# Delta rule: 16-row diagonal blocks inverted together on VectorE, doubling from 16 rows; convolution taps on VectorE alone

## The chip, the cores and the metric

The kernel runs on one core of one Trainium2 chip. The metric is the device time of one execution in microseconds; three executions of the kernel before gave 2950.22, 2953.05 and 2955.62 us, median 2953.05 us. Profiles are of one execution. The engines go by the profile's names: PE is TensorE's matmul, PEld its weight load, DVE is VectorE, ACT ScalarE, POOL GpSimd, SP SyncE (here: the queue that issues nearly all DMAs).

## What is computed

Two layers of a diffusion block (512 latent and 256 context tokens of width 1024: latent attention, a conformer branch with a 31-tap depthwise convolution, a short convolution, an MLP of width 4096), then two layers of a hybrid block on 512 tokens: gated delta rule, pooling and sparse attention, three branches with gates. All in float32. The change is in the first block's convolutions and in the delta rule:

```python
lmat = where(strict, einsum('nbhid,nbhjd->nbhij', k_beta, kc) * decay, 0)
tmat = triangular_solve(eye + lmat, eye, lower=True, unit_diagonal=True)
u = einsum('nbhij,nbhjd->nbhid', tmat, v_beta)
w = einsum('nbhij,nbhjd->nbhid', tmat, k_beta * exp(gc)[..., None])
```

and, of the conformer branch, `u = a * sigmoid(g)`, then a depthwise convolution with 31 taps plus a bias, a layer norm and a SiLU. The reference takes chunks of 64 rows; the kernel takes 4 chunks of 128 rows for each of 4 heads.

## The kernel before, in words

Matmuls of the projections run as three products of float32r parts: every weight tile is loaded by SP into a raw buffer, ACT casts it to the high part (`split`, L335) and DVE, or POOL where `pool=True`, subtracts to get the low part (L336). `fm` (L371) multiplies one 128-column weight tile with all tokens in 8 steps of three products (L382); `mm3` (L365) does the same for other products (L367 to L369). Matmuls on plain float32 data show as two records each.

The order of the work is made in three stages. Generators yield their own cost, and `Weave` (L211) runs whichever has the smallest clock, each at a rate of its own. A rehearsal of the whole program gives buffers their places. Then the framework's scheduler sets the order within each engine's queue; each engine and SP take their queue in that order, and semaphores carry the waits between them.

**First block.** For each layer `conv_proj` (L739) makes ten products, two times two for the gated input of the 31-tap convolution (`u`, L760) and two times three for the short convolution (L784 to L793). Each product loads and splits its own weight tile just before its matmuls; in the three-part loop the subtract is on POOL. `conv_taps` (L800) does the taps of two groups of 128 channels, 798 columns wide in layer 0 and 512 in layer 1: 24 of 30 taps as one multiply-add on DVE (L822); every fifth goes as a scaled copy on ACT (L815), which POOL adds up (L819), and one add on DVE (L824) joins them. Taps, projection and attention are woven at L1309, the taps at rate 1.1.

**Second block.** In each layer `second_layer` (L1967) weaves a chain, delta rule and then sparse attention at rate 1.25, with the choice of keys (`select_keys`, a long row of DVE instructions) and with `fill`: delta inputs, pooling, `sparse_proj` 0, `gated` of branch 1, `sparse_proj` 1, `gated` 0, `gated` 2. `delta` (L1555) takes the four chunks in turn. `head(n)` (L1569) transposes k and q, makes decay factors (L1585 to L1590) and the strictly lower matrix `Lw` (L1602), for four heads side by side as [128, 4, 128]. POOL then multiplies `Lw` with seven masks (L1609), one for each doubling level of block size 1, 2, 4 to 64. The inverse starts as identity minus level 0 on DVE (L1706). Each of six further levels does, for four heads, X minus Y times (Lm times X): four matmuls (L1719), a copy on ACT (L1720), four matmuls (L1725), a subtract on DVE (L1726), and, but for the last, a transpose of X into Y, four transposes (L1711) and a copy (L1712). While chunk n doubles, the head of chunk n+1 and the step of chunk n-1 (`step`, which uses the inverse and carries the state) are run between its pieces (`aside`). What each piece takes on the chain's clock stands in `STEPS` (L1553).

## Time and profile before

| | |
|---|---|
| median of three executions | 2953.05 us (2950.22 to 2955.62) |
| profiled execution | 2958.29 us, span of its instructions 2956.2 us |
| PE busy | 2824.0 us, 96% of the span |
| DVE busy | 1657.3 us, 56% |
| ACT busy | 1164.2 us, 39% |
| POOL busy | 576.7 us, 20% |
| granted PE clock, mean | 0.981 |

A row of instructions names line, engine, operation, output and inputs, shape and count, then busy time, mean duration and the engine's idle time ahead of them with what ended it. Durations of matmuls overlap, since they are pipelined: the cost of one is read from the distance between starts. A line number is that of the kernel before unless said otherwise; the changed kernel's lines stand one to some hundred further down.

### The profile page before, as it was taken

The page shows a single profiled execution, that of the slowest core. Times are in us where ns is not written, and L with a number is a line of the kernel's source. Part 1 is how long each engine was busy: PE and PEld are TensorE (multiplying, and loading weights), DVE is VectorE, ACT ScalarE, POOL GpSimd, SP SyncE. Part 2 cuts the span into 40 slices and gives each one's busy share as a digit, 9 for nine tenths or more (in the row PEclk, how much of TensorE's full clock was granted, in tenths as well). Part 3 has the DMA queues.
Part 4 walks back from the last instruction along what each step waited for, and adds up shares of the span by engine and source line. Part 5 has one row for each costly group of instructions (what it writes and reads, how often), then busy time and mean ns, then how long its engine had stood idle before and what let it go on. Part 6 is the DMA issues. An engine that isn't in the chain of part 4 may idle for free. (4 is left out here: it accounts for less than half of the span.)

```text
span 2956.2 us, 39081 instructions
## 1 busy us (share of the span) xinstructions
PE 2824.0 (96%) x15247; PEld 2341.5 (79%) x15247; DVE 1657.3 (56%) x2705; ACT 1164.2 (39%) x2260; POOL 576.7 (20%) x726
## 2 busy tenths in 40 slices
PE   6989999999999889999999999899999999999999
PEld 4867777888888767778888777798888878888887
DVE  4785652333334696554444787574543786675542
ACT  5337643222222527643233544343332543343431
POOL 2434220000000243210000124420311033412211
PEclk9989999999999889999999999999999999999999
DMA  6233344322121423542322511233233410232332
GB/s 218 56 96 121 119 162 132 93 59 77 58 62 58 131 76 108 185 139 83 96 86 92 155 44 30 61 83 90 72 105 99 136 34 24 65 95 72 87 107 79
DMA packets 319329, 276.62 MB, mean 94 GB/s; under 512 B 16868, under 2 KB 260776, under 8 KB 319144
## 3 DMA queue, kind: packets, MB, share of 16 engines
q1 hardware_dynamic: 318170, 271.90, 30.6%
q8 instruction: 120, 1.97, 0.3%
q0 software_dynamic: 704, 2.13, 0.2%
q14 instruction: 65, 0.53, 0.1%
q10 hardware_dynamic: 270, 0.09, 0.0%
HBM read 258.06 MB, written 13.66 MB: 92 GB/s over the span
## 5 line engine op out<-in xcount | busy, mean ns | idle before, releaser
L382 PE MATMUL bank<-at_r,at_r 128*128 128x512 f32 (+1 forms) x5568 | 1233.4, 376 | 18.6 <-POOL at_r L336 7.0
L382 PEld LDWEIGHTS bank<-at_r,at_r 128*128 128x128 f32 x5568 | 966.3, 191 | 201.0 <-issue 8.3
L336 DVE TENSOR_TENSOR at_r<-at_f,at_r 128x1024 fp32r<-128x1024 f32 (+5 forms) x436 | 476.0, 1098 | 467.1 <-ACT at_r L335 346.7
L367 PE MATMUL bank<-at_r,at_r 128*128 128x512 f32 (+5 forms) x1832 | 669.3, 366 | 17.8 <-DVE at_r L495 12.3
L335 ACT CAST at_r<-at_f 128x1024 fp32r<-128x1024 f32 (+6 forms) x450 | 414.2, 929 | 677.3 <-PE bank L369 176.1
L368 PE MATMUL bank<-at_r,at_r 128*128 128x512 f32 (+5 forms) x1832 | 658.9, 360 | 0.1
L369 PE MATMUL bank<-at_r,at_r 128*128 128x512 f32 (+5 forms) x1832 | 657.3, 359 | 0.0
L367 PEld LDWEIGHTS bank<-at_r,at_r 128*128 128x128 f32 x1832 | 349.4, 191 | 91.4 <-issue 15.1
L368 PEld LDWEIGHTS bank<-at_r,at_r 128*128 128x128 f32 x1832 | 350.4, 191 | 47.2 <-DVE at_r L336 1.4
L369 PEld LDWEIGHTS bank<-at_r,at_r 128*128 128x128 f32 x1832 | 349.4, 191 | 47.9 <-issue 1.0
L448 POOL MEMSET at_f<- 128x1 f32 x34 | 3.0, 98 | 873.7 <-PE bank L382 840.1
L515 POOL TENSOR_SCALAR at_f<-at_f,mx 128x768 f32<-128x768 f32 (+3 forms) x112 | 88.5, 791 | 364.6 <-DVE mx L514 335.7
L1217 DVE TENSOR_TENSOR at_f<-at_f,bank 128x512 f32<-128x512 f32 x120 | 81.7, 687 | 108.2 <-PE bank L369 108.2
L1172 ACT ACTIVATE at_f<-bank 128x768 f32<-128x768 f32 (+1 forms) x64 | 45.1, 704 | 202.5 <-PE bank L382 202.5
L1176 DVE TENSOR_TENSOR at_f<-at_f 128x768 f32<-128x768 f32 (+1 forms) x64 | 52.6, 822 | 89.8 <-ACT at_r L1175 89.8
L1609 POOL TENSOR_TENSOR at_f<-at_f,at_f 128x512 f32<-128x512 f32 x56 | 85.2, 1556 | 35.0 <-DVE at_f L1602 35.0
L512 DVE TENSOR_REDUCE mx<-bank 128x1 f32<-128x768 f32 (+1 forms) x80 | 67.4, 847 | 28.9 <-PE bank L369 28.7
L1952 POOL TENSOR_TENSOR at_f<-at_f 128x512 f32<-128x512 f32 x32 | 47.0, 1468 | 184.3 <-DVE at_f L1951 165.9
L336 DVE TENSOR_TENSOR at_r<-bank,at_r 128x256 fp32r<-128x256 f32 (+3 forms) x124 | 59.2, 483 | 35.5 <-ACT at_r L335 34.9
L822 DVE SCALAR_TENSOR_TENSOR at_f<-at_f,at_f 128x798 f32<-128x798 f32 x48 | 73.7, 1553 | 0.9
L513 ACT ACTIVATE at_f<-bank,mx 128x768 f32<-128x768 f32 (+1 forms) x80 | 65.6, 821 | 13.7 <-DVE mx L512 13.1
L335 ACT CAST at_r<-bank 128x256 fp32r<-128x256 f32 (+3 forms) x124 | 51.7, 424 | 46.5 <-PE bank L369 12.8
(292 smaller groups left out, 3233.9 us busy)
## 6 DMA issues: line engine op xcount, KB each, us to landing
at_f<-in_w_in_dram SPq DMA_DIRECT2D x148, 512.0 KB
at_f<-in_w_mod_dram SPq DMA_DIRECT2D x96, 512.0 KB
at_f<-in_w_mlp_in_dram SPq DMA_DIRECT2D x64, 512.0 KB
at_f<-in_w_mlp_out_dram SPq DMA_DIRECT2D x64, 512.0 KB
at_f<-d SPq DMA_DIRECT2D x28, 512.0 KB
at_f<-in_w_branch_dram SPq DMA_DIRECT2D x48, 256.0 KB
d<-at_f SPq DMA_DIRECT2D x22, 512.0 KB
at_f<-in_w_o_dram SPq DMA_DIRECT2D x16, 512.0 KB
```

What stands on the lines that cost most here:

```text
L335: self.nc.scalar.copy(hi, src)
L336: (self.nc.gpsimd if pool else self.nc.vector).tensor_tensor(lo, src, hi.bitcast(F32), op=OP.subtract)
L367: mm(ps, L[1], R[0], start=start, stop=False)
L368: mm(ps, L[0], R[1], start=False, stop=False)
L369: mm(ps, L[0], R[0], start=False, stop=stop)
L382: mm(ps[:, o:o + b - a], w[x][:, k], hl[y][:, k, a:b], start=k == 0 and j == 0, stop=k == nk - 1 and j == 2)
L512: nc.vector.tensor_reduce(mx[:, 0:1], ps, axis=AX, op=OP.max, negate=True)
L513: nc.scalar.activation(P, ps, AF.Exp, bias=mx[:, 0:1], accum_out=mx[:, 1:2])
L515: nc.gpsimd.tensor_scalar(P, P, mx[:, 2:3], 1.0, op0=OP.mult, op1=OP.mult)
L822: nc.vector.scalar_tensor_tensor(a, x, w, a, op0=OP.mult, op1=OP.add)
L1217: nc.vector.tensor_tensor(y, y, ps[t], op=OP.add)
L1609: nc.gpsimd.tensor_tensor(h["Lm"][lv], Lw, B2(self.mk[:, 4 + lv]), op=OP.mult)
```

## The change

Three things change.

The delta rule: the heads of all four chunks run first. Each writes, in 8 DMAs, its sixteen-row diagonal blocks to DRAM (512 runs of 64 bytes a head). One DMA brings the 128 blocks of 16 by 16 back, one block on each partition. Fifteen pairs of DVE instructions invert all of them at once, a copy transposes the result, two DMAs write result and transpose to DRAM, two read them back as [128, 16, 16] (2048 runs of 64 bytes each). `spread` puts them on the diagonal with a mask on POOL, as X and Y of each chunk, and makes the three level masks of block size 16, 32 and 64. The doubling has three levels instead of six after level 0. The clocks of the pieces (`STEPS`, `MOVE`) are larger. The mask table shrinks from 11 to 8.

The convolutions: all 30 taps on DVE at rate 1.6, no ACT copies and no POOL adds. `conv_proj` loads the weight of the next product ahead of the matmuls of this one and splits it after four of its eight steps, always with the subtract on DVE.

The fill: `gated` of branch 1 moves ahead of `sparse_proj` 0.

```diff
     def conv_proj(self, L):
...
+        def fetch():
+            raw, x = self.raw(8, 128), next(units)
+            nc.sync.dma_start(raw, x)
+            return raw
+        ready = [self.parts(fetch())]
+
+        def product():
+            w, ps = ready.pop(), self.P(T)
+            raw = fetch() if len(cols) > 1 else None
+            cols.pop()
+            for n, x in enumerate(self.fm(ps, w, src)):
+                if n == self.SPLIT and raw is not None:
+                    ready.append(self.parts(raw))
+                yield x
+            self.F(w)
+            return ps
...
-                w = self.w_fm(W, 0, 8, col + b * 128, pool=True)
-                ps = self.P(T)
-                yield from self.fm(ps, w, src)
-                self.F(w)
+            for part in range(3):
+                ps = yield from product()
...
             for s in range(1, 31):
-                x, w = u[:, s:s + n], c["cw"][:, s, b:b + 1]
-                if s % self.SIDE == 1 and s < 30:
...
-                nc.vector.scalar_tensor_tensor(a, x, w, a, op0=OP.mult, op1=OP.add)
+                nc.vector.scalar_tensor_tensor(a, u[:, s:s + n], c["cw"][:, s, b:b + 1], a, op0=OP.mult, op1=OP.add)
                 yield n / 960.0
-            nc.vector.tensor_tensor(a, a, side, op=OP.add)
...
-            W = Weave().add(self.conv_taps(L), 1.1).add(proj).add(self.attention(L))
+            W = Weave().add(self.conv_taps(L), 1.6).add(proj).add(self.attention(L))
...
-    STEPS = (0.62, 0.52, 1.35, 0.31)
+    STEPS, MOVE = (1.1, 1.4, 0.9), 4.0
...
-            h["Lm"] = [A() for _ in range(7)]
-            for lv in range(7):
-                nc.gpsimd.tensor_tensor(h["Lm"][lv], Lw, B2(self.mk[:, 4 + lv]), op=OP.mult)
-            F(Lw)
...
+            for b in range(8):
+                q = slice(16 * b, 16 * b + 16)
+                nc.sync.dma_start(rows[0].rearrange("(g b i) j -> b i g j", b=8, i=16)[b][:, 4 * n:4 * n + 4], Lw[q, :, q])
...
+        def blocks():
+
+            Lc, Z, tmp = (self.A(16, 16) for _ in range(3))
+            nc.sync.dma_start(Lc, rows[0].rearrange("(m i) j -> m i j", i=16))
+            nc.gpsimd.memset(Z, 0.0)
+            nc.gpsimd.memset(Z.rearrange("p c i -> p (c i)")[:, 0:256:17], 1.0)
+            yield self.MOVE
+            for i in range(1, 16):
+                nc.vector.tensor_tensor(tmp[:, :i, :i], Z[:, :i, :i], Lc[:, i:i + 1, :i].to_broadcast([128, i, i]),
+                                        op=OP.mult)
+                nc.vector.tensor_reduce(Z[:, :i, i], tmp[:, :i, :i], axis=AX, op=OP.add, negate=True)
+                yield 0.3
+            nc.vector.tensor_copy(tmp, Z.rearrange("p c i -> p i c"))
+            for r, x in zip(rows[1:], (Z, tmp)):
+                nc.sync.dma_start(r.rearrange("(m i) j -> m i j", i=16), x)
+            F(Lc, Z, tmp)
+            yield self.MOVE
+            for r in rows[1:]:
+                d = self.A(16, 16)
+                nc.sync.dma_start(d, r.rearrange("(g p) j -> p g j", p=128))
+                diag.append(d)
+            yield self.MOVE
+
+        def spread(n, h):
+
+            h["XY"], h["Lm"] = [A(), A()], [A() for _ in range(3)]
+            mask = self.mk[:, 7:8].rearrange("p a (b i) -> p a b i", b=8)
+            for d, x in zip(diag, h["XY"]):
+                nc.gpsimd.tensor_tensor(x.rearrange("p e (b i) -> p e b i", b=8),
+                                        d[:, 4 * n:4 * n + 4, None].to_broadcast([128, 4, 8, 16]),
+                                        mask.to_broadcast([128, 4, 8, 16]), op=OP.mult)
+            for lv in range(3):
+                nc.gpsimd.tensor_tensor(h["Lm"][lv], h["L"], B2(self.mk[:, 4 + lv]), op=OP.mult)
...
+        for n in range(4):
+            for _ in head(n, hs[n]):
+                yield 1.2
+        yield self.MOVE
+        yield from blocks()
+        for _ in spread(0, hs[0]):
+            yield self.MOVE
...
-            Y, X, P1 = A(), A(), A()
-            nc.vector.tensor_tensor(Y, B2(self.ident), h["Lm"][0], op=OP.subtract)
+            (X, Y), P1 = h["XY"], A()
...
-            for lv in range(1, 7):
+            for lv in range(3):
...
             yield from self.pooling(l, hT, c, R)
+            yield from self.gated(l, hT, c, R, 1, first=True)
             R["rg"] = self.rope_gains(l)
             yield from self.sparse_proj(l, hT, R, 0)
-            yield from self.gated(l, hT, c, R, 1, first=True)
             yield from self.sparse_proj(l, hT, R, 1)
```

How this moves instructions shows at three places. In these rows `bank` is PSUM, `at_..._f` and `at_..._r` are buffers of float32 and float32r, `d_...` is DRAM scratch.

PE at the start of the first chunk's doubling in the second block's first layer; L382 is the fill's product, L1711, L1719 and L1725 are transposes, first and second matmuls of a level. Before:

```order
L1711 MATMUL bank<-ident,at_8_f 128x128 x4
L382 MATMUL bank<-at_64_r,at_16_r 128x512 x3
L1719 MATMUL bank<-at_8_f 128x128 x4
L382 MATMUL bank<-at_64_r,at_16_r 128x512 x4
L1725 MATMUL bank<-at_8_f 128x128 x4
L382 MATMUL bank<-at_64_r,at_16_r 128x512 x8
L1711 MATMUL bank<-ident,at_8_f 128x128 x4
L1719 MATMUL bank<-at_8_f 128x128 x4
L382 MATMUL bank<-at_64_r,at_16_r 128x512 x6
L1725 MATMUL bank<-at_8_f 128x128 x4
L382 MATMUL bank<-at_64_r,at_16_r 128x512 x6
```

The same place in the changed kernel, whose line 383 is the fill's product and whose lines 1762, 1768 and 1756 are first matmuls, second matmuls and transposes:

```order
L383 MATMUL bank<-at_64_r,at_16_r 128x512 x23
L1762 MATMUL bank<-at_8_f 128x128 x4
L383 MATMUL bank<-at_64_r,at_16_r 128x512 x6
L1768 MATMUL bank<-at_8_f 128x128 x4
L383 MATMUL bank<-at_64_r,at_16_r 128x512 x9
L1756 MATMUL bank<-ident,at_8_f 128x128 x4
L1719 MATMUL bank<-ident,at_8_f 128x128 x4
L383 MATMUL bank<-at_64_r,at_16_r 128x512 x6
L1762 MATMUL bank<-at_8_f 128x128 x4
L383 MATMUL bank<-at_64_r,at_16_r 128x512 x3
```

Level 0's transposes are gone, the first matmuls come straight on a long run of the fill's products, and between pieces of a level there are 6 to 9 products of the fill where there were 3 to 8, or none.

SP's queue in the same stretch, the changed kernel: L353 loads weights, L1611 writes the diagonal blocks of one head, L1680 reads all blocks, L1691 writes results, L1696 reads them spread. Before, L352 had this stretch to itself but for tables.

```order
L1611 DMA d_12608<-at_8_f 16x4x16 x8
L353 DMA at_16_f<-in_w_in_dram 128x8x128
L1611 DMA d_12608<-at_8_f 16x4x16 x8
L353 DMA at_16_f<-in_w_in_dram 128x8x128
L353 DMA at_2_f<-in_pool_w_dram 128x128
L353 DMA at_16_f<-in_w_in_dram 128x8x128
L1611 DMA d_12608<-at_8_f 16x4x16 x8
L1680 DMA at_4_f<-d_12608 128x256
L353 DMA at_16_f<-in_w_in_dram 128x8x128 x2
L353 DMA at_2_f<-in_pool_w_dram 128x128
L1691 DMA d_12609<-at_4_f 128x256
L1691 DMA d_12610<-at_4_f 128x256
L1696 DMA at_4_f<-d_12609 128x16x16
L1696 DMA at_4_f<-d_12610 128x16x16
```

Weight loads of the fill (L353) stand behind DMAs that wait for VectorE (L1611, L1691) or for a landing (L1680, L1696).

VectorE and POOL in `conv_proj` of the first block's first layer, where the split of a weight is L336 before and L337 now. POOL before:

```order
L336 TENSOR_TENSOR at_16_r<-at_16_f,at_16_r 128x1024
L819 TENSOR_TENSOR at_13_f<-at_13_f 128x798 x3
L336 TENSOR_TENSOR at_16_r<-at_16_f,at_16_r 128x1024
L819 TENSOR_TENSOR at_13_f<-at_13_f 128x798 x2
L336 TENSOR_TENSOR at_16_r<-at_16_f,at_16_r 128x1024 x2
L819 TENSOR_TENSOR at_13_f<-at_13_f 128x798
```

POOL has none of these rows now. VectorE now, where the tap is L826, the gated input L779 and the first tap L824:

```order
L337 TENSOR_TENSOR at_16_r<-at_16_f,at_16_r 128x1024
L337 TENSOR_TENSOR at_12_r<-bank,at_12_r 64x768
L824 TENSOR_SCALAR at_13_f<-at_13_f,at_1_f,at_2_f 128x798
L946 TENSOR_TENSOR at_12_f<-bank,at_12_f 64x768
L337 TENSOR_TENSOR at_12_r<-bank,at_12_r 64x768
L826 SCALAR_TENSOR_TENSOR at_13_f<-at_13_f,at_1_f 128x798
L337 TENSOR_TENSOR at_12_r<-at_12_f,at_12_r 128x768
L826 SCALAR_TENSOR_TENSOR at_13_f<-at_13_f,at_1_f 128x798
L337 TENSOR_TENSOR at_16_r<-at_16_f,at_16_r 128x1024
L826 SCALAR_TENSOR_TENSOR at_13_f<-at_13_f,at_1_f 128x798 x12
L779 SCALAR_TENSOR_TENSOR at_13_f<-at_12_f,bank 128x512
L779 SCALAR_TENSOR_TENSOR at_13_f<-at_12_f,bank 128x256
L826 SCALAR_TENSOR_TENSOR at_13_f<-at_13_f,at_1_f 128x798 x6
```

The splits and the adds have left POOL; on VectorE the weight splits (128x1024) now stand between the taps, each ahead of the product that needs it.

## Rows read from the trace of the kernel before

**Rows 1.** The page, busy time: engine, us (share of the span), instructions.

```profile
span 2956.2 us, 39081 instructions
...
PE 2824.0 (96%) x15247; PEld 2341.5 (79%) x15247; DVE 1657.3 (56%) x2705; ACT 1164.2 (39%) x2260; POOL 576.7 (20%) x726
```

**Rows 2.** Who PE waited for, whole span: us, times, longest us.

```profile
PE bank L1711 <- DVE at_f L1726: 8.2, 8, 2.4
PE bank L1640 <- ACT at_f L1634: 7.7, 2, 4.2
...
PE bank L1725 <- ACT at_f L1720: 7.1, 7, 3.1
PE bank L382 <- POOL at_r L336: 7.0, 1, 7.0
PE bank L382 <- DVE at_r L336: 6.2, 1, 6.2
...
PE bank L601 <- DVE at_f L788: 3.9, 1, 3.9
...
PE bank L367 <- DVE at_f L793: 2.5, 1, 2.5
...
PE bank L367 <- DVE at_f L784: 2.2, 1, 2.2
```

**Rows 3.** Stretch, length, busy us: PE, PEld, DVE, ACT, POOL; clock, DMA share, GB/s.

```profile
100.00:200.00 100.00, 86.61 (x462) 73.54 (x461) 94.05 (x80) 27.47 (x39) 45.29 (x25) 0.90 0.18 53
1040.00:1115.00 75.00, 64.06 (x279) 50.92 (x277) 68.79 (x76) 23.36 (x40) 36.83 (x30) 0.90 0.30 81
1770.00:1935.00 165.00, 149.44 (x995) 131.84 (x996) 108.23 (x205) 63.10 (x128) 71.43 (x69) 0.97 0.17 47
2425.00:2610.00 185.00, 170.66 (x1196) 153.59 (x1195) 119.38 (x230) 72.19 (x160) 75.55 (x85) 0.98 0.17 48
```

**Rows 4.** Groups by line and shape: count, busy us, mean ns.

```profile
L1725 PE MATMUL bank<-at_f 128*128 128x128 f32 x384 | 56.5, 292 | 10.0 <-ACT at_f L1720 7.1 <-DVE at_f L1602 2.6
L1719 PE MATMUL bank<-at_f 128*128 128x128 f32 x384 | 51.0, 275 | 0.5 <-ACT at_f L1712 0.3 <-issue 0.2
...
L1711 PE MATMUL bank<-ident,at_f 128*128 128x128 f32 x192 | 30.0, 279 | 10.6 <-DVE at_f L1726 8.2 <-DVE at_f L1706 2.3
```

**Rows 5.** PE in the doubling, in order of time: start us, us, count, idle ahead.

```profile
1781.85 1.05 PE L1719 MATMUL bank<-at_f 128*128 128x128 f32 x8
...
1797.62 0.66 PE L1711 MATMUL bank<-ident,at_f 128*128 128x128 f32 x4 [2.43 <-DVE at_f L1726]
```

**Rows 6.** Busy time and granted clock around two waits of PE, columns as in rows 3.

```profile
162.40:175.00 12.60, 5.55 (x18) 4.78 (x18) 12.60 (x11) 2.32 (x3) 8.71 (x7) 0.59 0.40 127
...
1852.00:1861.20 9.20, 6.15 (x21) 5.30 (x22) 1.64 (x3) 1.86 (x4) 0.00 (x0) 0.63 0.24 65
```

**Rows 7.** One line each, taps: duration ns min/median/max, first and last start.

```profile
L822 DVE SCALAR_TENSOR_TENSOR at_f<-at_f,at_f x48: 1035/1052/3121, 103.7 to 188.2; 128x798 f32<-128x798 f32 x48
L822 DVE SCALAR_TENSOR_TENSOR at_f<-at_f,at_f,at_f x48: 735/752/2877, 1044.6 to 1105.6; 128x512 f32<-128x512 f32 x48
```

**Rows 8.** Groups by line and shape: taps and weight splits.

```profile
L336 DVE TENSOR_TENSOR at_r<-at_f,at_r 128x1024 fp32r<-128x1024 f32 x310 | 384.9, 1246 | 407.1 <-ACT at_r L335 303.6 <-PE bank L368 42.4 <-PE bank L382 26.2
...
L822 DVE SCALAR_TENSOR_TENSOR at_f<-at_f,at_f 128x798 f32<-128x798 f32 x48 | 73.7, 1553 | 0.9
...
L336 POOL TENSOR_TENSOR at_r<-at_f,at_r 128x1024 fp32r<-128x1024 f32 x12 | 33.0, 2756 | 15.9 <-ACT at_r L335 12.2 <-DVE at_f L788 3.7
```

**Rows 9.** One line, the masks on POOL: duration ns min/median/max.

```profile
L1609 POOL TENSOR_TENSOR at_f<-at_f,at_f x56: 1260/1300/2283, 1777.1 to 2541.5; 128x512 f32<-128x512 f32 x56
```

**Rows 10.** DMA issues: KB each, median us from issue to landing.

```profile
d<-at_f POOLq DMA_DIRECT2D x4, 8.0 KB, 2.0
```

**Rows 11.** DMA packets of 1619.9 to 1622.2 us, share of 16 engines.

```profile
DMA packets 361, 0.10 MB, mean 45 GB/s; under 512 B 287, under 2 KB 361, under 8 KB 361
...
q1 hardware_dynamic: 361, 0.10, 18.0%
```

More of the change, by code (lines that the diff above doesn't have):

```diff
@@ L65, in _shape_tables @@
     mk[:, 3] = np.where(j > i, -big, 0)
-    for n, b in enumerate((1, 2, 4, 8, 16, 32, 64)):
+    for n, b in enumerate((16, 32, 64)):
         mk[:, 4 + n] = (i // (2 * b) == j // (2 * b)) & (i // b % 2 == 1) & (j // b % 2 == 0)
+    mk[:, 7] = i // 16 == j // 16
     t["mk"] = mk
@@ L744, in conv_proj @@
         U = UMIX if wide else 542
+        cols = [c0 + b * 128 for b in range(2) for c0 in (672, 416)]
+        cols += [c0 + b * 128 for b in range(2) for c0 in (1184, 1440, 928)]
+        units = iter([W[:, x:x + 128].rearrange("(k p) n -> p k n", p=128) for x in cols])
+        def fetch():
[13 more added lines that the diff above has]
+            return ps
         for b in range(2):
@@ L769, in conv_proj @@
             cs = self.A(T)
-            for part, col in enumerate((1184, 1440, 928)):
-                w = self.w_fm(W, 0, 8, col + b * 128, pool=True)
-                ps = self.P(T)
-                yield from self.fm(ps, w, src)
-                self.F(w)
+            for part in range(3):
+                ps = yield from product()
                 if part == 0:
@@ L1685, in step @@
             yield
-        h = {}
-        for _ in head(0, h):
-            yield 1.0
+        def blocks():
[19 more added lines that the diff above has]
+            yield self.MOVE
@@ new lines, in spread @@
+        def spread(n, h):
[7 more added lines that the diff above has]
+                nc.gpsimd.tensor_tensor(h["Lm"][lv], h["L"], B2(self.mk[:, 4 + lv]), op=OP.mult)
+            F(h["L"])
+            yield
+            if n:
+                qe, h["qeT"], h["kbg"] = A(), A(), A()
+                nc.gpsimd.tensor_tensor(qe, qn[:, n], H2(g["eg"][:, n]), op=OP.mult)
+                nc.gpsimd.tensor_tensor(h["kbg"], kn[:, n], H2(g["bg"][:, n]), op=OP.mult)
+                yield
+                pq = self.P(4, 128)
+                for e in range(4):
+                    nc.tensor.transpose(pq[:, e], qe[:, e], self.ident)
+                nc.scalar.copy(h["qeT"], pq)
+                F(pq, qe)
+            if n < 3:
+                h["kd"] = A()
+                nc.gpsimd.tensor_tensor(h["kd"], kn[:, n], H2(g["ek"][:, n]), op=OP.mult)
+            yield
@@ L1690, in delta @@
+        rows, diag = [self.dram([2048, 16]) for _ in range(3)], []
+        hs = [{} for _ in range(4)]
+        for n in range(4):
[5 more added lines that the diff above has]
+            yield self.MOVE
         side = []
         for n in range(4):
-            nxt = {}
+            h = hs[n]
             if n < 3:
-                side.append(head(n + 1, nxt))
+                side.append(spread(n + 1, hs[n + 1]))
@@ L1727, in delta @@
                 F(p)
[L1728 to L1729 removed]
+                yield aside(self.STEPS[1])
+                if lv < 2:
                     flip(X, Y)
[L1731 removed]
+                    yield aside(self.STEPS[2])
             F(Y, P1, h["Lm"])
```

45 lines of the change are left out of this document (8 added, 37 removed).

## The prediction

> **What bounds the kernel.** I read the busy times first: PE is busy 2824.0 of 2956.2 us, 96%, every other engine 56% or less [rows 1]. So PE work that is taken out shortens the time one for one, as long as no new wait of PE takes its place, and the change takes out PE work. Next I read who PE waits for [rows 2]: no single wait over 8.2 us, and those that the change touches are of two kinds. In the doubling of the delta rule PE waits for VectorE's subtract (L1711 behind L1726) and for ACT's copy (L1725 behind L1720); in the first block's projections it waits for a weight's subtract (L382 behind POOL's and VectorE's L336) or for VectorE's short convolution, which frees a bank or a buffer (L784, L788, L793). Then the stretches where these lie [rows 3]: in the projections PE is busy 86.61 of 100 and 64.06 of 75 us while VectorE is at 94.05 and 68.79, so VectorE is the limit there; in the delta stretches PE is busy 149.44 of 165 and 170.66 of 185 us, with VectorE at some 65%. The granted clock is 0.90 in the projections, since it falls to its lower level (1.2 of 2.4 GHz) after a longer wait of PE [rows 6].
>
> **PE work removed.** A level needs, for 4 heads, 4 chunks and 2 layers, 32 first and 32 second matmuls. Levels fall from 6 to 3, so 96 and 96 matmuls go; each is two records, as 384 records for 192 matmuls show [rows 4]. Eight records take 1.05 us, of which the last one's own length is 0.275 us: seven distances of 0.111 us [rows 4, 5]. 384 records by 0.111 us are 42.6 us. Transposes fall from 6 to 2 for each chunk: 4 by 4 by 4 by 2, 128 records. Four take 0.66 us, less the last one's 0.279 us: three distances of 0.127 us, against 0.111 for a matmul record. I take 0.12, 15.4 us (14.2 to 16.3). Together 58 us, all on PE, which has other work waiting at both sides of them.
>
> The transposes of qe, k and q, the Gram products and the steps are all kept, only moved: no PE cost.
>
> **Waits of the doubling removed.** PE stands idle 15.6 and 14.3 us in the two delta stretches [rows 3]. Of these 15.3 us are the level's own: 8.2 in 8 waits and 7.1 in 7 [rows 2]. Half of the levels are left, and the pieces stand further apart (6 to 9 products of the fill between them, where there were 3 to 8 or none). I leave 4 us and count 11 us gained. One of them, at 1852 us, also cost clock: 0.63 over 9.2 us is 3.4 us of full speed [rows 6], and part of that fell into the idle time; 3 us. The 7.7 us of L1640 belong to the step, which stays. Together 14 us (between 0 and 18.3).
>
> **Waits added.** Three of four heads move to the front. For a head VectorE does four 512-wide instructions, by 0.752 us for an unhindered instruction of that width [rows 7], and four 128-wide ones, which I put at 0.28 us (at least a quarter of 0.752, so 0.19): 4.1 us, 12.3 us for three. The fifteen pairs work on at most 225 columns; no row has such a shape. Above each is bounded by the 0.752 us of 512 columns, 22.6 us in all, below by nothing; nearer to the small end, since the mean pair has 83 columns: 0.2 us each, 6 us. About 5 us of the first chunk's old subtracts leave the same stretch. So VectorE has some 13 us more to do in the first half of a stretch where it is at 65% on the mean but has fuller places. PE's share of that is between 0 and 13 us a layer; I take 5, because splits of weights are queued behind these instructions, though they lie ahead of their use.
>
> Then the way through DRAM. A landing takes 2.0 us for 8 KB [rows 10]. The spread reads have 2048 packets each. 361 small packets took 18.0% of 16 engines' 2.3 us, 6.6 us, 18 ns each [rows 11]; 2048 by 18 ns over 16 engines is 2.3 us. So write 2.0, read 4.3, and masks on POOL of 1.30 us each [rows 9]: one before the first matmul, and up to three before the second operand is there: 7.6 to 10.2 us, or 13 with POOL's longest, 2.28 us. The program plans four times 4.0 by rate 1.25, 20 us of fill, between write and first level. That covers it unless VectorE is late by 7 to 12 us when it ends the last pair; in the queue of PE the first level stands at a fixed place behind a run of products, and what is late there PE waits for. Between 0 and 10 us a layer with the clock; I take 3.
>
> The DMA share is low here, 0.17 in both delta stretches [rows 3]; 6144 packets of 64 bytes a layer by 18 ns over 16 engines are 7 us of it, spread over some 40 us. Nothing on PE. Of 64-byte writes no row tells. The Trainium skill, DMA: Bandwidth & Descriptors, section Specifications, says that below 512 bytes the engine does a read-modify-write; no row shows what that costs. If it doubled the packets' time, a spread read or a head's write would land some 2.3 us later, and the time would be at most 4.6 us longer than mine.
>
> POOL is relieved: 20 mask products a layer for 28 [rows 9], and no masks during the heads. That costs PE nothing and frees nothing on PE. VectorE's copies, ACT's copies of the removed levels: off PE's path but for the waits counted above. Waits added: 8 a layer for the two sides 5 and 3, 16 us for both.
>
> **The projections.** The waits are 7.0 and 3.9 us in layer 0, 6.2, 2.5 and 2.2 in layer 1 [rows 2], 21.8 us; behind the 7.0 us PE worked 5.55 us at about half speed, 2.8 us lost [rows 6]. Two more stops of a like kind lie there (3.9; 6.2), and 2.5 and 2.2 together: four times some 2.2 to 2.8, 9 us. At most 31 us to gain. Does VectorE have room? Taps: 48 by the mean of 1553 ns were 73.7 us [rows 8]; the median is 1052 ns and the longest 3121 [rows 7], so a few are held up by something. Without POOL's adds and splits beside them I take the median: 60 by 1.052 is 63 us. Six splits of 1.246 us come from POOL, where they took 2.756 [rows 8]: 7.5 us. So VectorE in layer 0 goes from 94.05 to 94.05 - 73.7 + 63 + 7.5 = 91 us, and rate 1.6 spreads the taps into the attention that follows. Still nearly full, but the split of a weight now stands four steps of a product ahead of its use. I take two thirds of 31, 20 us (0 to 31). If the median were not reached, 60 by 1.553 is 93 us, and VectorE would be at 121 of 100: then this term is a loss of some 15 us.
>
> The order of `gated` 1 and `sparse_proj` 0 changes nothing in the sum: the same work, covered by the fill on both sides.
>
> **Sum.** 2958.3 us for the profiled execution, less 58, less 14, plus 16, less 20, is 2882 us. That execution lies 5.2 us above the median of 2953.05; against the median the sum gives **2877 us**.
>
> **Rivals.**
> 1. *The new waits eat a good part.* VectorE is so late with the fifteen pairs that PE stands 20 us a layer at the first level, and the projections give 5 us: 2953 - 58 - 14 + 40 - 5 = 2916; 2916 to 2945. For it: VectorE already sets the pace where it is over 90% [rows 3]. Against: 20 us of fill are planned in between.
> 2. *The queue of SP turns it slower.* In each layer SP now waits in nine places ahead of weight loads (four heads, one read of all, two writes, two reads). If a weight behind each is late, PE waits for landing 2.0, cast and subtract 1.25 each, and 3 us of clock: 7.5 us. 18 times that is 135 us, less my 76 of gain: 3012 us. It decides from 11 of 18 places on. Against: buffers are filled well ahead, and the view of PE's waits names no DMA in these stretches [rows 2].
> 3. *All waits go.* No new wait, projections at 31: 2953 - 58 - 18 - 31 = 2846 and below.
> 4. *No change*: the freed PE time is only idle, because the chain through DRAM and the doubling is longer than the fill. Then the inverse would come too late for `gated` 0; before, whole delta stretches of 165 and 185 us fitted [rows 3], so hardly.
>
> **Chances.** Forecast 0.74, rival 1 0.13, rival 2 0.05, rival 3 0.06, rival 4 0.02. The range takes the forecast's bounds, from rival 3's edge to rival 1's: 2846 to 2916. No change means within 0.2%, about what a measurement of this kernel can tell: faster 0.93, same 0.02, slower 0.05.
>
> **What would show it.** First matmuls and second matmuls of the doubling at 192 records each and its transposes at 64; PE's busy time in the delta stretches lower by 58 us for the same fill. PE's wait at the first level (line 1762, behind POOL) of about 3 us a layer: over 8 it is rival 1. Taps 60 and 60, at a median near 1052 and 752 ns with few long ones; no wait of L382 for a subtract in the projections. PE waiting for casts or subtracts behind late weights in many places would be rival 2. Wrong outright: PE idle over 45 us in a delta stretch, or VectorE's taps at a mean over 1.5 us.

## The result and the profile after

The changed kernel takes 2877.94 us (median of 4 executions, 2875.69 to 2879.93) against 2952.36 us for the kernel before in the same session: a ratio of 0.9747, with a 95% interval of 0.973 to 0.9764. The forecast was 2877. Line numbers below are those of the changed kernel, unless another is named.

The busy times, which answer to [rows 1]: PE has lost 68.5 us, POOL 99 us, and ACT 51 us.

```profile
PE 2755.5 (96%) x14735; PEld 2278.5 (79%) x14735; DVE 1623.9 (56%) x2767; ACT 1113.5 (39%) x2180; POOL 477.6 (17%) x680
```

I cut the execution into two blocks at the first transpose (line 465, before: 464) of the norm ahead of layer 2: 1637.5 us before, 1613.5 us after. The projections lie in the first block, the delta rule in the second. The table of windows, first of the kernel before, then after (start and end, length, busy time and count of each engine, granted clock, DMA share):

```profile
core 0: us, PE busy (x) PEld busy (x) DVE busy (x) ACT busy (x) POOL busy (x), PEclk, DMA share, GB/s
0.00:1637.50 1637.50, 1557.70 (x8143) 1259.39 (x8143) 867.06 (x1268) 650.36 (x1165) 266.66 (x340) 0.97 0.34 106
1637.50:2956.20 1318.70, 1266.29 (x7105) 1082.14 (x7105) 790.20 (x1437) 513.84 (x1095) 310.02 (x387) 0.99 0.28 79
```

```profile
0.00:1613.50 1613.50, 1549.68 (x8142) 1252.12 (x8142) 852.19 (x1301) 632.45 (x1141) 195.71 (x308) 0.98 0.35 107
1613.50:2878.20 1264.70, 1205.84 (x6593) 1026.41 (x6593) 771.74 (x1466) 481.00 (x1039) 281.85 (x373) 0.99 0.30 83
100.00:200.00 100.00, 97.03 (x568) 81.34 (x570) 91.82 (x111) 25.41 (x46) 14.03 (x24) 1.00 0.25 71
1020.00:1095.00 75.00, 69.10 (x335) 54.98 (x333) 70.08 (x103) 24.25 (x44) 9.62 (x23) 1.00 0.39 110
1770.00:1820.00 50.00, 44.84 (x189) 35.26 (x188) 49.30 (x124) 13.06 (x20) 15.33 (x14) 0.93 0.26 60
```

The first block is 24.0 us shorter, the second 54.0. In the second, PE has 512 matmul records less (7105 to 6593, which is 384 of matmuls and 128 of transposes) and is busy 60.5 us less; the time in which PE is not busy went from 52.4 to 58.9 us. So the second block's gain is work, and its waits did not shrink in the sum. The records of the doubling that are left:

```profile
L1768 PE MATMUL bank<-at_f 128*128 128x128 f32 x192 | 25.5, 275 | 1.4 <-ACT at_f L1763 1.0 <-POOL at_f L1705 0.4
L1762 PE MATMUL bank<-at_f 128*128 128x128 f32 x192 | 25.4, 275 | 0.7 <-POOL at_f L1705 0.7
...
L1756 PE MATMUL bank<-ident,at_f 128*128 128x128 f32 x64 | 10.0, 279 | 4.3 <-DVE at_f L1769 4.3
```

In the projections PE is now busy 97.03 of 100 us at full clock and 69.10 of 75, where it was 86.61 and 64.06 at 0.90 [rows 3].

Whom PE waits for now, against [rows 2] (engine, line, whom it waited for, us in total, times, longest):

```profile
PE bank L1943 <- POOL at_f L516: 22.6, 18, 2.3
...
PE bank L368 <- ACT at_r L336: 11.2, 8, 2.8
...
PE bank L1756 <- DVE at_f L1769: 4.3, 4, 1.6
...
PE bank L1768 <- ACT at_f L1763: 1.0, 1, 1.0
...
PE bank L1762 <- POOL at_f L1705: 0.7, 1, 0.7
```

The doubling's own waits are 4.3 and 1.0 us, the first level's on POOL 0.7 for X and 0.4 for Y. PE's largest wait in the whole kernel is a new one: the transposes of the sparse attention (line 1943) wait for the softmax's product on POOL. The kernel before had 2.9 us of it:

```profile
PE bank L1901 <- POOL at_f L515: 2.9, 4, 1.0
```

The 11.2 us of line 368 behind ACT's cast are new too. Six of the eight stops, 7.9 us, lie around the fifteen pairs, three in each layer, and there ACT casts an input of the fill's pooling that VectorE (L1812) has finished late. One of them, on PE and on ACT:

```profile
1812.89 0.79 PE L368 MATMUL bank<-at_r,at_r 128*128 128x512 f32 x1 [2.29 <-ACT at_r L336]
...
1812.22 0.62 ACT L336 CAST at_r<-at_f 128x512 fp32r<-128x512 f32 x1 [5.31 <-DVE at_f L1812]
```

The taps (operation, count, shortest, median and longest in ns, first and last start), as in [rows 7]:

```profile
L826 DVE SCALAR_TENSOR_TENSOR at_f<-at_f,at_f x60: 1030/1050/1970, 111.1 to 198.8; 128x798 f32<-128x798 f32 x60
L826 DVE SCALAR_TENSOR_TENSOR at_f<-at_f,at_f,at_f x60: 730/747/1200, 1026.5 to 1093.3; 128x512 f32<-128x512 f32 x60
```

The fifteen pairs of layer 2, on DVE from the first product to the transposing copy, with the mask product of X behind them on POOL (start, us, engine, line, operation; in brackets the idle time ahead and what ended it):

```profile
1787.37 0.65 DVE L1685 TENSOR_TENSOR at_f<-at_f 128x1 f32<-128x1 f32 x1
...
1813.40 0.37 DVE L1687 TENSOR_REDUCE at_f<-at_f 128x15 f32<-128x225 f32 x1
...
1814.30 0.37 DVE L1689 COPY at_f<-at_f 128x256 f32<-128x256 f32 x1
...
1818.97 5.24 POOL L1705 TENSOR_TENSOR at_f<-at_f,at_f 128x512 f32<-128x512 f32 x4 [2.06 <-DMA at_f<-d]
```

They take 26.4 us to the last reduction, where the program plans fifteen steps of 0.3 at rate 1.25, 5.6 us. VectorE was busy 49.3 of 50 us there, and only a part of that was the pairs: from the first product to the copy they took some 9 us, the choice of keys (L1493, L1494) 10 and the fill 13, in durations that overlap a little. From the copy's end to X's mask it is 4.3 us, write and read together.

### The profile page after: what moved, and what is told of

The parts are those of the page before. It is cut to its first block, busy times and chain, and to the rows that moved or that the text cites. A ratio compares the mean times of both kernels' runs of the same rounds, so it can differ in the third digit from the quotient of the medians.

```text
span 2878.2 us, 37990 instructions
## 1 busy us (share of the span) xinstructions
PE 2755.5 (96%) x14735; PEld 2278.5 (79%) x14735; DVE 1623.9 (56%) x2767; ACT 1113.5 (39%) x2180; POOL 477.6 (17%) x680
## 5 line engine op out<-in xcount | busy, mean ns | idle before, releaser
L383 PE MATMUL bank<-at_r,at_r 128*128 128x512 f32 (+1 forms) x5568 | 1214.8, 374 | 2.4 <-ACT at_r L495 2.2
L337 DVE TENSOR_TENSOR at_r<-at_f,at_r 128x1024 fp32r<-128x1024 f32 (+6 forms) x448 | 494.1, 1113 | 486.3 <-ACT at_r L336 380.7
L336 ACT CAST at_r<-at_f 128x1024 fp32r<-128x1024 f32 (+4 forms) x450 | 412.9, 929 | 622.4 <-PE bank L370 190.7
L1175 ACT ACTIVATE at_f<-bank 128x768 f32<-128x768 f32 (+1 forms) x64 | 45.1, 705 | 258.7 <-PE bank L383 258.7
L516 POOL TENSOR_SCALAR at_f<-at_f,mx 128x768 f32<-128x768 f32 (+3 forms) x112 | 95.3, 853 | 239.8 <-DVE mx L515 221.7
L1179 DVE TENSOR_TENSOR at_f<-at_f 128x768 f32<-128x768 f32 (+1 forms) x64 | 52.6, 822 | 101.4 <-ACT at_r L1178 101.4
L1994 POOL TENSOR_TENSOR at_f<-at_f 128x512 f32<-128x512 f32 x32 | 50.4, 1575 | 178.7 <-DVE at_f L1993 156.5
L336 ACT CAST at_r<-bank 128x256 fp32r<-128x256 f32 (+4 forms) x124 | 51.5, 425 | 68.6 <-PE bank L1943 33.4
L337 DVE TENSOR_TENSOR at_r<-bank,at_r 128x256 fp32r<-128x256 f32 (+4 forms) x124 | 58.9, 483 | 29.7 <-ACT at_r L336 28.7
L1002 PE MATMUL bank<-ident,at_f 128*128 128x128 f32 x416 | 63.0, 279 | 5.6 <-ACT at_f L1006 2.9
L602 PE MATMUL bank<-at_f,at_f 128*32 128x512 f32 x384 | 60.7, 619 | 5.3 <-DMA at_f<-in_w_mod_dram 5.3
```

The lines of the kernel that those rows point to most:

```text
L336: self.nc.scalar.copy(hi, src)
L337: (self.nc.gpsimd if pool else self.nc.vector).tensor_tensor(lo, src, hi.bitcast(F32), op=OP.subtract)
L383: mm(ps[:, o:o + b - a], w[x][:, k], hl[y][:, k, a:b], start=k == 0 and j == 0, stop=k == nk - 1 and j == 2)
L516: nc.gpsimd.tensor_scalar(P, P, mx[:, 2:3], 1.0, op0=OP.mult, op1=OP.mult)
L602: nc.tensor.matmul(ps[q:q + 32], self.sT[:, k], raws[j - 1 + k // 2 % 2][:, k % 2], start=k < 4, stop=k >= 4)
L1002: nc.tensor.transpose(pt[:, k], P[:, k * 128:(k + 1) * 128], self.ident)
```

## The experiments

For each run the two blocks are shown as in the result: the profiled execution up to layer 2's norm, and the rest of its span. That is one execution, from 6.0 us below its kernel's median (`both_late`) to 9.6 above it (`delta_only`), so its own time stands beside the median.

| run | median us | profiled us | ratio to before, 95% | first block | second block |
|---|---|---|---|---|---|
| before | 2952.36 | 2958.29 | | 1637.5 | 1318.7 |
| changed | 2877.94 | 2879.93 | 0.973 to 0.9764 | 1613.5 | 1264.7 |
| proj_only | 2934.53 | 2934.14 | 0.9927 to 0.9957 | 1615.1 | 1317.3 |
| delta_only | 2908.5 | 2918.11 | 0.9839 to 0.988 | 1647.2 | 1269.2 |
| before_places | 2941.37 | 2946.59 | 0.9939 to 0.9972 | 1636.7 | 1308.2 |
| delta_places | 2901.91 | 2907.99 | 0.9809 to 0.9841 | 1640.7 | 1265.5 |
| after_places | 2880.67 | 2887.42 | 0.9738 to 0.9771 | 1623.7 | 1262.0 |
| twice | 2910.59 | 2908.43 | 0.9846 to 0.9879 | 1610.8 | 1295.9 |
| move_short | 2868.59 | 2869.87 | 0.9703 to 0.9732 | 1609.0 | 1259.2 |
| old_order | 2894.71 | 2898.07 | 0.9793 to 0.9823 | 1617.7 | 1278.7 |
| both_late | 2868.1 | 2862.07 | 0.9703 to 0.9735 | 1607.7 | 1252.7 |
| short_late | 2872.42 | 2875.78 | 0.9711 to 0.974 | 1612.9 | 1261.2 |
| old_taps | 2892.03 | 2891.49 | 0.978 to 0.9813 | 1628.5 | 1261.0 |
| old_fetch | 2902.55 | 2901.8 | 0.9819 to 0.9848 | 1637.0 | 1263.1 |

**The two halves.** `proj_only` is the kernel before with the change's hunks in `conv_proj` and `conv_taps`, shown ahead, and

```diff
-    SIDE, FIRST = 5, 6
+    FIRST, SPLIT = 6, 4
...
-            W = Weave().add(self.conv_taps(L), 1.1).add(proj).add(self.attention(L))
+            W = Weave().add(self.conv_taps(L), 1.6).add(proj).add(self.attention(L))
```

`delta_only` has all the other hunks: `delta`, `STEPS`, the mask table and the order of the fill.

> The kernel before with the change's part in the first block alone: fetch ahead, splits in mid-product, all taps on VectorE at rate 1.6; the delta rule stays as before. Theory (the two parts lie in different blocks and add up; in the profile after, the first block is 14.9 us shorter in layer 0 and 8.2 us in layer 1 up to the norm behind the attention): about 2930 us, 2927 to 2934. Rival (the gain there comes from the second block's weights being ahead, or from the mask table that is 1.5 KB smaller): under 10 us of gain, 2943 us or more.

> The kernel before with the change's part in the second block alone: blocks of 16 rows through DRAM, three levels, gated 1 ahead of sparse_proj 0; the projections stay as before. Theory (in the profile after, layers 2 and 3 are some 54 us shorter: 58 us of PE work gone, clock 2 to 3 us back, waits the same in the sum): about 2899 us, 2895 to 2903, and its gain and that of the other part together give the 74.4 us of the whole change within 4 us. Rival (one part helps the other through the clock or through weights that are fetched earlier): the two gains together miss the whole by more than 8 us.

They gained 19.1 and 45.1 us: 64 of the 74 that the whole gains, so the theory's sum missed by 10, which is the rival's sign; both medians lie above the theory's ranges, by 0.5 and 5.5 us. By blocks the parts do add up where they act: the first block is 22.4 us shorter in the one, the second 49.5 us in the other. What is missing is that the first block of `delta_only` is 9.7 us longer than before (the expectations below put it at 12), though its code is the same. That left three causes: one part helps the other; the places of the buffers, which the planner gives to the whole program at once; or this one execution, which lies 9.6 us above its kernel's median.

**Other places for the buffers.** The same edit to three kernels:

```diff
-SPARES, TRIES = (16.0, 8.0, 4.0, 2.0, 1.0, 0.0), 30
+SPARES, TRIES = (8.0, 4.0, 2.0, 1.0, 0.0), 30
```

> The kernel before, with only the margin changed at which the planner begins to place buffers (8 for 16); the work is the same, the buffers lie elsewhere, and the scheduler's order moves a little with them. The two halves alone gained 19 and 45 us, 10 us less than the whole, and the first block of the second half alone, with the same code as before, was 12 us longer in its profile. Theory (places alone move a kernel by that much): off the 2952 us by 4 us or more, up or down. Rival (the halves help each other, places don't matter): 2949 to 2956 us.

> The second block's half of the change alone, with the planner's margin 8 for 16. Theory (its first block was unlucky in its places): up to 12 us less than 2908.5, 2896 to 2904 us, the difference in the first block; or, as places are a matter of chance, off by 4 us or more to the other side. Rival (the old projections lose by the new second block whatever the places): 2905 to 2912 us.

> The changed kernel with the planner's margin 8 for 16. Theory (fetch ahead and free taps leave the first block so much slack that places matter less): within 4 us of 2878. Rival (places move it as much as they seem to move the half): off by 4 to 12 us, 2866 to 2874 or 2882 to 2890 us.

Places alone moved the kernel before by 12.1 us, clear of its interval (0.9939 to 0.9972). The second half moved by 6.6 us and the changed kernel by 2.7 us, both as their theories had it, and neither clear of noise: each ratio is known to some 5 us either way. In the changed kernel's trace one block moved by +10.2 us and the other by -2.7, so its blocks are not steadier than the others'. So the 10 us by which the halves miss the whole are within what places and noise do; that the parts help each other is neither shown nor ruled out by them. A single comparison here is good to some 10 us. With the margin 8 for 16 on both sides the change is worth 60.7 us instead of 74.4. I therefore compare blocks, and take runs with the same code in a block together. First block with the old projections: 1636.7 to 1647.2 in 4 runs, mean 1640.5; with both new parts 1607.7 to 1623.7 in 8 runs, mean 1613.8. Second block with the old delta rule: 1308.2 to 1318.7 in 3 runs, mean 1314.7; with the new one unaltered 1261.0 to 1269.2 in 6 runs, mean 1264.3. By these means the change is worth 26.7 us in the first block and 50.4 in the second. The first is probably too much: the four profiled executions with the old projections lie 6.7 us above their kernels' medians on the mean and the eight with the new ones 1.0, so I take 21 to 27 us. In the second block the two groups lie 3.6 and 3.9 us above theirs, and 50.4 stands. PE's idle time in the first block parts the groups as well: 79.8 to 92.2 us in the four, 62.7 to 68.3 in the eight.

**The price of the removed records.**

```diff
-                for e in range(4):
+                for e in (0, 1, 2, 3) * 2:
                     mm(p[:, e], h["Lm"][lv][:, e], X[:, e], start=True, stop=True)
```

and likewise for the second matmul.

> The changed kernel with each of the levels' 192 matmuls (96 first, 96 second) issued twice into the same bank, the second time over the first; the values are the same. It puts back as many matmul records as the change took out, 384, and no wait or copy. Theory (a record costs PE 0.111 us wherever it stands, because PE is the bound there): plus 42.6 us, 2920 us, 2914 to 2926. Rival 1 (the chain is the bound in the doubling, and freed PE time was half idle): plus 21 us or less, 2899 us or less. Rival 2 (later copies make new waits and lower the clock): plus 55 us or more, 2933 or more.

```profile
1610.80:2906.70 1295.90, 1242.75 (x6977) 1066.18 (x6977) 772.54 (x1466) 483.26 (x1038) 277.99 (x374) 1.00 0.29 81
```

384 more records (6593 to 6977) made PE busy 36.9 us more in the second block, and the kernel 32.7 us slower, 3 us under the theory's range and about midway between the theory's 42.6 and rival 1's 21; nothing of rival 2 shows. But the record itself costs what was forecast. A group of first matmuls, in the changed kernel and here:

```profile
1822.58 1.05 PE L1762 MATMUL bank<-at_f 128*128 128x128 f32 x8
...
1823.25 1.95 PE L1762 MATMUL bank<-at_f 128*128 128x128 f32 x16
```

Eight more take 0.90 us, 0.1125 us each, 43 us for 384. The block grew by 31.2 us only, since other things shrank beside it: PE's idle time by 5.7 us (58.9 to 53.2; the wait of line 368 for a cast went from 11.2 to 2.9), and its other busy time by some 6 us, at a clock of 1.00 where the changed kernel has 0.99. Why these shrank was not tried; places, or the order that the scheduler makes, can do it. So the missing 10 us do not need rival 1, and do not rule it out either.

**Less fill ahead of the first level.** 
```diff
-    STEPS, MOVE = (1.1, 1.4, 0.9), 4.0
+    STEPS, MOVE = (1.1, 1.4, 0.9), 0.5
```

> The changed kernel with MOVE 0.5 for 4.0: 4 times 3.5 by 1.25, 17 us, of the fill between the last head and the first level go behind the first level. After the change the fifteen pairs take 27 us from first to last, since VectorE is busy 49.3 of 50 us there, X comes 8 us after the last pair, and PE waits 0.7 us for it. Theory A (the way through DRAM and the crowded VectorE are hidden by that fill alone): the pairs end only some 5 us sooner, PE waits 8 to 15 us a layer at the first level for POOL's X, with the clock 2893 to 2912 us. Theory B (VectorE is late because of the fill's own work, which now comes later; then the pairs move ahead by as much): waits under 3 us a layer, 2875 to 2883 us.

The pairs move ahead as theory B had it; the median is 6 us under its range, and the waits at the level are a little over its 3 us a layer. In layer 2 the transposing copy and X's mask:

```profile
1802.08 0.38 DVE L1689 COPY at_f<-at_f 128x256 f32<-128x256 f32 x1
...
1807.52 7.63 POOL L1705 TENSOR_TENSOR at_f<-at_f,at_f 128x512 f32<-128x512 f32 x5 [0.28 <-DMA at_f<-d]
```

```profile
PE bank L368 <- ACT at_r L336: 4.2, 4, 1.7
...
PE bank L1768 <- POOL at_f L1705: 3.5, 2, 1.8
...
PE bank L1762 <- POOL at_f L1705: 3.2, 2, 1.7
...
PE bank L1756 <- DVE at_f L1769: 2.0, 3, 1.1
```

With 17 us of fill less, the pairs end 12 us earlier (2.1 us of it because the delta rule begins earlier), since VectorE has less of the other work between them: 3.5 us of the choice of keys and 10 of the fill, where it was 10 and 13. PE's waits for X and Y grow from 1.1 to 6.7 us in both layers together, its wait for the pooling's casts falls with the crowding (line 368, 11.2 to 4.2), as does that for VectorE's subtract, and the second block is 5.5 us shorter. That is at the edge of what places do, so I claim only that these 17 us of fill bought nothing.

**The order of the fill.** `old_order` against the changed kernel, and `both_late`, which keeps the new order:

```diff
-            yield from self.gated(l, hT, c, R, 1, first=True)
             R["rg"] = self.rope_gains(l)
             yield from self.sparse_proj(l, hT, R, 0)
+            yield from self.gated(l, hT, c, R, 1, first=True)
```

```diff
-        while ("sp", pr) not in R or "selected" not in R:
+        while ("sp", 1) not in R or "selected" not in R:
```

> The changed kernel with gated 1 put back behind sparse_proj 0. In the profile after, PE waits 22.6 us in 18 places for the softmax's product on POOL in the sparse attention of pair 0, which now runs beside sparse_proj 1; before, it was 2.9 us, beside gated 1. Theory A (the new order makes these waits, and buys nothing else): they go, and with them about 15 us: 2863 us, 2858 to 2868. Theory B (gated 1 was moved ahead because sparse_proj 0 loads VectorE while the fifteen pairs run): the waits in the sparse attention go, but PE then waits at the first level for POOL's X and Y, 5 to 12 us a layer more than the 0.7 us after: 2873 to 2890 us. Theory C (the shorter chain makes the waits, not the order): the waits stay near 20 us, 2876 to 2880.

> The changed kernel with its order kept, but the sparse attention of pair 0 begins only when sparse_proj 1 is done too, so that both pairs run beside gated 0. Theory (the 22.6 us of waits for the softmax's product come from its place beside sparse_proj 1, whose own chains take POOL and whose PE work lies in longer pieces): waits for it under 6 us, 11 to 17 us gained, 2861 to 2867 us. Rival (gated 0 with some 66 us of PE work doesn't cover both pairs, and gated 2 waits for the last one): PE stands idle at the end of the sparse attention instead, no gain or a loss, 2876 to 2890 us.

In `old_order` the wait of line 1943 falls to 1.1 us, yet the second block is 14.0 us longer than in the changed kernel, outside the scatter of places. The time is lost where theory B had it, but by another wait, and mostly through the clock; the median is 5 us above its range. Between 1830 and 1955 us:

```profile
PE bank L1756 <- DVE at_f L1769: 5.6, 4, 3.7
PE bank L1628 <- DVE at_f L1769: 3.0, 1, 3.0
...
1830.00:1955.00 125.00, 111.09 (x793) 104.65 (x794) 68.83 (x125) 45.50 (x126) 47.20 (x67) 0.93 0.23 63
```

Not X and Y are late (0.9 and 1.3 us in the whole kernel), but VectorE's subtract between two levels (L1769), beside `sparse_proj` 0. VectorE is not full there: it is busy 68.83 of 125 us, 55%, against 53% in the changed kernel's stretch below. Ahead of the wait of 3.0 us its queue shows

```profile
1848.19 0.42 DVE L1889 TENSOR_TENSOR at_f<-at_f 128x256 f32<-128x256 f32 x1 [5.34 <-POOL at_f L1888]
1849.54 0.42 DVE L1882 TENSOR_TENSOR at_f<-bank,rstd 128x256 f32<-128x256 f32 x1 [0.93 <-POOL rstd L392]
1849.88 0.68 DVE L1769 TENSOR_TENSOR at_f<-at_f,bank 128x512 f32<-128x512 f32 x1
```

The last matmul ahead of this subtract began at 1842.81 us in a group of 1.06 us. The subtract stood in VectorE's queue behind two instructions of `sparse_proj` 0 that waited for POOL, and VectorE was idle meanwhile. The granted clock is 0.93 over 125 us, where it is 1.00 in the changed kernel's stretch from 1820 to 1930:

```profile
1820.00:1930.00 110.00, 107.92 (x679) 94.74 (x678) 58.55 (x100) 44.46 (x92) 28.36 (x28) 1.00 0.27 78
```

7% of 125 us are 8.8 us in layer 2 alone. In the second block PE is busy 12.6 us more than in the changed kernel (1218.4 against 1205.8) and idle about as long (60.3 against 58.9), so the loss is nearly all clock.

`both_late` shows what the softmax's waits can cost. In both layers its waits are

```profile
PE bank L1867 <- DVE at_f L1889: 9.7, 9, 5.0
...
PE bank L1756 <- DVE at_f L1769: 6.0, 6, 2.3
...
PE bank L1943 <- POOL at_f L516: 2.4, 3, 1.3
```

so 20.2 us of line 1943 are gone, some 8 come back at line 1867, and the second block is 12.0 us shorter, below all six of the unaltered one. Gated 0 covers both pairs. Its median is 9.8 us under the changed kernel's, within what places can do and 1 us above the theory's range. The block is that of an execution 6.0 us below the kernel's median, where the changed kernel's is 2.0 above. PE's busy time in it is the same (1205.7 us); its idle time is 47.0 us, against 52.6 to 59.8 in the six. So up to 12 us are the waits', in this one execution.

> The changed kernel with two edits that each gained when alone: MOVE 0.5 (2868.6 us) and both pairs of the sparse attention behind sparse_proj 1 (2868.1 us). Theory (they act at different places, the fifteen pairs and the sparse attention; about 4 us of either gain lay in the first block, whose program they hardly touch, and is not counted twice): 2860 us, 2856 to 2865. Rival (with less fill ahead of the levels the delta rule ends earlier, so that the sparse attention finds other fill anyway): 2866 to 2870 us, no more than either alone.

The two edits together gave 2872.42 us: neither the sum nor better than either alone, as the rival said (a little above its range), with the second block at 1261.2. There the wait of line 1943 is gone too (2.1 us), and yet the block is no shorter than with `MOVE` 0.5 alone (1259.2). So the price of the softmax's waits is not settled: 12 us in `both_late`, nothing here. 2868 us is the best that I have, with either edit, and the three are not told apart from each other beyond places.

**What helped in the projections.** `old_taps` is the changed kernel with the taps of before (12 products on ACT, adds on POOL, rate 1.1); `old_fetch` is the changed kernel with the lines back that the diff removes in `conv_proj`:

```diff
-                ps = yield from product()
+                w = self.w_fm(W, 0, 8, col + b * 128, pool=True)
+                ps = self.P(T)
+                yield from self.fm(ps, w, src)
+                self.F(w)
```

> The changed kernel with the taps as before (48 on VectorE, 12 as products on ACT with adds on POOL, rate 1.1); the fetch ahead stays. Theory A (POOL's adds slow VectorE: the mean tap was 1553 and 1121 ns with them and is 1069 and 754 without): the means come back to 1450 ns or more and 1050 or more, VectorE has some 7 us more to do in layer 0, and the projections lose 5 to 14 us: 2884 to 2892 us. Theory B (the fetch ahead alone removes the waits, since a split four steps ahead bears a late VectorE): 2875 to 2881 us. Theory C (POOL's splits made the taps slow, not its adds): means under 1200 ns, and no loss.

> The changed kernel with the projections' weights as before (fetched and split when a product is set up, six of them split on POOL in layer 0); the taps stay all on VectorE at rate 1.6. Theory A (both halves of the change are needed: POOL's splits of 2.76 us stand in front of their products): waits of L383 for a subtract are back, 5 to 14 us with the clock, 2884 to 2892 us. Theory B (taps alone free VectorE and thereby the splits): 2875 to 2881 us. Of the taps: if POOL's splits beside them are what slowed them, their mean in layer 0 is over 1300 ns; if POOL's adds were, under 1150.

The means of a tap (shape, count, busy us, mean ns), first `old_taps`, where only adds run on POOL beside them, then `old_fetch`, where only splits do:

```profile
L838 DVE SCALAR_TENSOR_TENSOR at_f<-at_f,at_f 128x798 f32<-128x798 f32 x48 | 61.3, 1297 | 0.7
L838 DVE SCALAR_TENSOR_TENSOR at_f<-at_f,at_f,at_f 128x512 f32<-128x512 f32 x48 | 45.2, 963 | 0.6
```

```profile
L811 DVE SCALAR_TENSOR_TENSOR at_f<-at_f,at_f 128x798 f32<-128x798 f32 x60 | 71.3, 1188 | 1.5
L811 DVE SCALAR_TENSOR_TENSOR at_f<-at_f,at_f,at_f 128x512 f32<-128x512 f32 x60 | 51.5, 868 | 1.2
```

The medians lie at the upper edge of theory A's range (`old_taps`) and 11 us above it (`old_fetch`). Neither theory of the tap was whole: its mean is 1069 and 754 ns with neither, 1297 and 963 with the adds, 1188 and 868 with the splits, and 1553 [rows 8] with both. Against the mean of 1613.8 the first block is 14.7 us longer with the old taps and 23.2 with the old fetch; the old of both is 26.7 longer. By medians it is 14.1 and 24.6 us. PE's idle time in the first block is 81.8 and 77.3 us, far nearer to the old projections' than to the new ones'. So both halves are needed, and the taps alone win almost nothing: 3.5 us, less than places do. The fetch ahead and the move of the splits from POOL to VectorE were put back together, so which of these two counts is open. With the old taps a split that stands four steps ahead is late all the same (`old_taps`, whole span):

```profile
PE bank L383 <- DVE at_r L337: 14.2, 3, 10.3
```

With the old fetch PE's largest wait in the projections is another than theory A named, for the short convolution on VectorE (`old_fetch`):

```profile
PE bank L368 <- DVE at_f L794: 8.7, 2, 4.4
```

## Why the prediction was right, and where it was not

**PE work removed, 58 us.** Right: busy time fell by 60.5 us in the second block, with exactly the 512 records counted; 192 are left for each matmul of a level and 64 for its transposes. The price of a matmul record was right as well, 0.1125 us in `twice` for 0.111. Giving 384 of them back cost the kernel 32.7 us and not 43, for reasons that lie beside the records.

**Waits of the doubling, 14 us.** Right: 15.3 us of subtract and copy became 5.3, where I left 4. But "the 7.7 us of L1640 belong to the step, which stays" was wrong: no such wait is left in the trace after. Nor are two that I did not count, of 2.6 and 2.3 us (L1725 behind L1602, L1711 behind L1706 [rows 4]): 12.6 us of unforeseen savings with it.

**Waits added, 16 us.** The sum was nearly right and its parts were not. The wait for X at the first level is 0.7 us in both layers, not 3 a layer. The lateness of VectorE was real, 26 us for the pairs in place of 6, but PE paid for it in the fill: 7.9 us behind the casts of the pooling's inputs in both layers. In layer 2 these and the subtracts behind them are the 5.2 us in which PE was not busy between 1770 and 1820 us, at a clock of 0.93. I held that 20 us of fill cover the way through DRAM; `move_short` shows that the work woven in with the pairs, fill and choice of keys, is what made them late, and that the way (4.3 us, expected 6.3) hardly needs it.

**"The order of `gated` 1 and `sparse_proj` 0 changes nothing in the sum"** is the step that failed. It moves two things of opposite sign: it spares the second block 14 us, net (`old_order`), and it puts the sparse attention of pair 0 beside `sparse_proj` 1, with 19.7 us more of waits, which cost up to 12 us (`both_late`) or nothing that shows (`short_late`). I had looked at PE's work only, which indeed doesn't change, and not at whose instructions stand ahead of the chain's in VectorE's and POOL's queues. The 19.7 us of unforeseen wait and the 12.6 of unforeseen savings partly cancelled in my sum; that much is luck.

**Projections, 20 us.** Right: 24.0 in the profile, 21 to 27 over places, where 31 was the bound. The taps reached the medians of 1052 and 752 ns (1050 and 747), VectorE is busy 91.82 us of the 100 where I had 91, and no wait of the projections' matmul (line 383) for a subtract is left. I did not see that the gain lies in the fetch ahead together with the taps, and hardly in the taps alone.

**Rivals.** Rival 1 had the mechanism (a late VectorE) and not its price, for the level stands behind the same late fill. Rival 2: of the 11.2 us for which PE waits on casts in the second block 7.9 are the pooling's inputs and not weights, so late weights can have cost 3.3 at most, nothing like 135. Of the 64-byte runs, for which I gave at most 4.6 us more: X's read of 2048 runs is issued at 1815.58 us, its mask starts 3.4 us later, within the 4.3 that I took. No run tells what a head's write of such runs costs, so the Trainium skill's rule (DMA: Bandwidth & Descriptors, section Specifications) stays neither shown nor refuted; nothing on PE waits for one.

That 2877 met 2877.94 is partly chance: other places of the buffers move either kernel by 3 to 12 us, and with the other margin the change gains 61 us.

## What to carry to other kernels

Price a reordering of fill by what it puts ahead of the chain in the queues of the chain's engines, and by what those instructions wait for, not by the bound engine's work or by busy shares: here it was worth 14 us with the same matmuls, and VectorE was 55% busy where it was late. Work woven between a short chain and its use is no cover if it runs on the chain's own engine; it is then what makes the chain late. Where one planner places all buffers, time the unchanged kernel with other places too before a gain of a few tenths of a per cent is believed, and compare stage by stage.

## What was not expected of the hardware

A VectorE tap slows when POOL works beside it, and not by a little in every tap: the median stays (1046 ns in `old_taps`, 1050 in the changed kernel), the longest rises from 1970 to 2700 ns beside POOL's adds (mean 2471 ns) and to 3069 beside POOL's splits (mean 2667 ns). First `old_taps`, then `old_fetch`:

```profile
L838 DVE SCALAR_TENSOR_TENSOR at_f<-at_f,at_f x48: 1034/1046/2700, 107.6 to 184.0; 128x798 f32<-128x798 f32 x48
...
L811 DVE SCALAR_TENSOR_TENSOR at_f<-at_f,at_f x60: 1031/1050/3069, 109.4 to 202.4; 128x798 f32<-128x798 f32 x60
```

In `old_taps` a tap that started at 166.45 us, 0.88 us into an add of 2.71 us, took 2.67 us and so ended 0.84 us after the add. The Trainium skill, SBUF — State Buffer, section Who interferes with whom, says that a VectorE instruction with two SBUF inputs contends with a GpSimd instruction that reads SBUF, and calls the contention an exclusive lock; this tap agrees, as it stood until the add was done.

The clock did not follow the length of PE's stops. Beside the pairs of the changed kernel the longest stop is 2.29 us in layer 2 and 2.20 in layer 3, and the clock is 0.89 in the one and 1.00 in the other; at the softmax eight stops of up to 2.31 us, 9.8 in all, left it at 0.97:

```profile
1800.00:1830.00 30.00, 27.39 (x119) 21.88 (x118) 27.67 (x62) 7.85 (x13) 12.11 (x11) 0.89 0.18 38
...
2400.00:2440.00 40.00, 35.40 (x152) 27.80 (x151) 37.75 (x103) 9.09 (x14) 12.77 (x13) 1.00 0.24 60
...
1990.00:2050.00 60.00, 50.18 (x379) 47.32 (x379) 34.34 (x78) 23.70 (x76) 22.48 (x40) 0.97 0.21 57
```

In `old_order` stops of 3.0 and 3.7 us, among others, went with 0.93 over 125 us. What decides between them was not tried.
